# Query parts stored by whole column tile and loaded by SyncE, bias loads issued by ACT, the inversion's diagonal copies split over DVE and ACT

## The chip, the cores and the metric

The kernel runs on one core of a Trainium2 chip. The core has five engines that work through their own instruction queues in order: TensorE (PE, matrix products into PSUM; its weight loads are shown apart, as PEld), VectorE (DVE), ScalarE (ACT), GpSimd (POOL) and SyncE (SP, which here only issues transfers). Transfers between the chip's main memory and on-chip memory are run by 16 DMA engines, whoever issues them. The metric is the device time of one execution in microseconds. Before the change three runs took 1245.56, 1245.53 and 1241.6 us; the median is 1245.53.

## The reference

One layer of an encoder over 1024 tokens of width 1024, float32, with two groups of heads that read the same normalised input through one input projection: windowed attention (8 query heads of 64, 2 key heads, a band of 128 tokens to each side with a relative bias and a sink logit) and a gated delta rule that runs forwards and backwards (4 heads of 128). Then an output projection, a feed-forward block with squared ReLU and a final normalisation.

```python
xn = _rmsnorm(h, norm_mix_w[l])
proj = xn @ w_in[l]
q_a, k_a, v_a, qkv_g, z_g, a_g, b_g = jnp.split(proj, SPLIT_POINTS, axis=-1)
attn = _windowed_gqa(q_a, k_a, v_a, band_bias, in_window, attn_sink[l])
gdn = _gdn_mixer(qkv_g, z_g, a_g, b_g, conv_w[l], ...)
h = h + jnp.concatenate([attn, gdn], axis=-1) @ w_out[l]
hn = _rmsnorm(h, norm_ffn_w[l])
h = h + jnp.square(jax.nn.relu(hn @ w_ffn_in[l])) @ w_ffn_out[l]
...
# attention, per block n of 128 queries against its 3-block band of keys
scores = jnp.einsum("bnqkgd,bnskd->bnkgqs", qb, kb) * (ATTN_HEAD_DIM ** -0.5)
scores = scores + bias
probs = jax.nn.softmax(jnp.concatenate([scores, sink_col], axis=-1), axis=-1)[..., :-1]
...
# delta rule, per chunk
a_mat = jnp.where(strict, beta[..., :, None] * kk * decay, 0.0)
t_mat = lax.linalg.triangular_solve(eye + a_mat, eye, left_side=True, lower=True)
```

## The kernel before, in words

Most products are run as three: each operand is split into a rounded high part and the remainder, and PE adds high by high, high by low and low by high (L127 to L129). ACT makes the high part (L122 for weights, L501 for queries), POOL the low one (L123, L502).

The program is a chain of phases, in each of which generators are woven together. Around the change, from about 220 to 580 us, there are two such phases.

In the first, one stream runs the last input projections (`proj_conv`, `proj_z`, then `proj_attn`, whose last part makes the queries), and the other prepares the delta rule: `prep`, `eliminate`, `diag_blocks` and rounds 0 and 1 of `invert`. In the second, one stream is `attention`, then the output projection; the other runs rounds 2 and 3 of `invert`, then the scan forwards (`scan`, 8 chunks) and backwards.

**Queries.** For each key head `kv` two column tiles `i` of 128 columns (two heads each) and two halves of 512 tokens are projected. DVE evacuates the product (L500), ACT casts to the high part (L501), POOL subtracts (L502). Both parts are stored to a scratch tensor `qad` in main memory, since scores want the high part of a head on 64 partitions and the low part on the other 64 (the matching keys are laid out in the same way, in `kh` and `kl`). Before the change a store moves one head's part (64 partitions, L506): eight evacuations, 32 stores, all on SP. `query(n, kv)` loads the four heads of one block of 128 tokens as one tile; the load (L600) is issued by POOL. The first query of each key head is asked for while the projections still run, later ones two steps ahead.

**Attention.** A step is one block `n` and one key head `kv`, 16 in all: (0,0), (0,1), (1,0) and so on. PE makes scores (L550, L551), DVE adds the bias and finds the maximum (L552), ACT takes the exponentials (L564), DVE sums and scales (L565 to L569, one quarter of the scaling on POOL), PE transposes (L579), ACT evacuates (L581), and PE multiplies by the values (L591), which DVE evacuates (L594) and SP stores to `mad` (L595).

**Bias.** Four tiles of two heads each (`bias_table`), every one loaded by four transfers (L535) on SP. Their buffers come from the tag `pg`, 24 buffers which all large tiles share; the four were operands of the projections before.

**Inversion.** `invert` makes the inverse of a triangular 128 by 128 matrix per head, chunk and direction `d`, 8 of each direction at once, in four rounds `i`. The result tile is cleared by POOL (L716), the 32 by 32 diagonal blocks are copied in (L720, eight copies of 32 partitions by 256 elements, which read with a stride), a first product (L726) is copied to SBUF by ACT (L729), a second pair of products (L736, L740) gives the blocks beside the diagonal (L745, L752 on DVE), four more copies on ACT (L750) complete the 64 by 64 blocks, and two products of 64 (L759, copied by ACT at L761, then L767) give the last quarter (L770).

**Scan.** For each chunk SP loads `kvd` (L798), `pd` (L800) and for each pair of chunks `ktd` and `qtd` (L786); PE's products are at L805.

**What sets the order.** The streams are written as generators with due times, and the framework then orders the instructions by a simulated timeline, engine by engine: the order of each engine's queue is fixed when the program is built. Waits between engines are semaphores. Transfers issued by SP and ACT share eight completion counters in turn, so each transfer waits, on the queue that issues it, until the one eight places earlier in the program has landed.

Of the kernel before, what the change touches and what calls it, by code (L numbers as in the profile page):

```python
# [9 lines left out]
F32 = mybir.dt.float32  # L10
F32R = mybir.dt.float32r
# [5 lines left out]
P = 128  # L17
SEQ = 1024
# [3 lines left out]
HALF = 512  # L22
# [55 lines left out]
class Block:  # L78
# [389 lines left out]
    def proj_attn(self):  # L468


        nc = self.nc
# [7 lines left out]
        for i, half, ps in self.pair(raws):  # L479
            tok = slice(half * HALF, (half + 1) * HALF)  # L480
            t = self.pt()
# [14 lines left out]
        for kv in range(2):  # L496
            raws = self.load_w(self.w_cols(w, C_AQ + 256 * kv, 256))
            for i, half, ps in self.pair(raws):
                q, qh = self.pt(), self.pt(dt=F32R)
                nc.vector.tensor_scalar(out=q, in0=ps, scalar1=0.125, scalar2=None, op0=ALU.mult)  # L500
                nc.scalar.copy(out=qh, in_=q)  # L501
                nc.gpsimd.tensor_tensor(out=q, in0=q, in1=qh.bitcast(F32), op=ALU.subtract)  # L502
                for part, t in enumerate((qh.bitcast(F32), q)):
                    o = 64 * (kv ^ part)
                    for g in range(2):
                        nc.sync.dma_start(out=self.qad[kv, 2 * i + g, o:o + 64, half * HALF:(half + 1) * HALF],  # L506
                                          in_=t[64 * g:64 * g + 64, :])
                if i == 1 and half == 0:
                    self.qs.append(self.query(0, kv))
                yield 5.2  # L510
# [16 lines left out]
    def bias_table(self):  # L527
        self.bias = []
        for b in range(4):
            t = self.pg((P, 2, 3 * P))  # L530
            for m in range(4):
                src = bass.AP(tensor=self.biasd.tensor,
                              offset=self.biasd.offset + 2 * b * 32 * 512 + P - 1 - 32 * m,
                              ap=[[511, 32], [32 * 512, 2], [1, 3 * P]])
                self.nc.sync.dma_start(out=t[32 * m:32 * m + 32], in_=src)  # L535
            self.bias.append(t)

    def attn_scores(self, n, kv, mx, q, mk):
# [58 lines left out]
    def query(self, n, kv):  # L597

        q = self.pt((P, 4, P), F32R)
        self.nc.gpsimd.dma_start(out=q, in_=self.qad[kv, :, :, n * P:(n + 1) * P].rearrange("g c t -> c g t").bitcast(F32R))  # L600
        return q

    def attention(self):
# [91 lines left out]
    def invert(self, tt, steps):  # L695


        nc = self.nc
        blk = lambda q: slice(32 * q, 32 * q + 32)
        ct, ctt = self.ct, self.ctt  # L700
# [5 lines left out]
        for i in steps:  # L706
            ns = slice(8 * i, 8 * i + 8)
# [7 lines left out]
                tt[d][i] = mk((P, 2, GH, P), F32) if mk else self.pg((P, 2, GH, P))  # L715
                nc.gpsimd.memset(tt[d][i].rearrange("p c h x -> p (c h x)"), 0.0)  # L716
            t = [flat(tt[d][i]) for d in range(2)]
            for d in range(2):
                for q in range(4):
                    nc.scalar.copy(out=t[d][blk(q), :, blk(q)], in_=ctt[d][blk(q), :, ns].rearrange("p x n -> p n x"))  # L720
            px = self.ps("psB", (P, 8, 32))
            for n in range(8):
                for j in range(2):
# [2 lines left out]
                        nc.tensor.matmul(px[blk(e), n, :], at[d][blk(s), n, blk(e)], ct[d][blk(s), :, 8 * i + n],  # L726
                                         start=True, stop=True)
            x32 = self.pt((P, 8, 32))
            nc.scalar.copy(out=x32, in_=px)  # L729
            yield 1.4  # L730
            pyt, py = self.ps("psB", (P, 8, 32)), self.ps("psB", (P, 8, 32))
            for n in range(8):
                for j in range(2):
# [9 lines left out]
            for d in range(2):  # L743
# [4 lines left out]
                for q in (a, b):  # L748
                    c = slice(32 * (q % 2), 32 * (q % 2) + 32)
# [2 lines left out]
                nc.vector.tensor_scalar(out=t64[blk(b), :, 32 * (a % 2):32 * (a % 2) + 32], in0=py[blk(b)], scalar1=-1.0,  # L752
                                        scalar2=None, op0=ALU.mult)
            yield 2.4
            px = self.ps("psB", (P, 8, 64))
            for n in range(8):
                for d in range(2):
# [491 lines left out]
    def build(self):  # L1249
        tc, nc = self.tc, self.nc  # L1250
        with (
# [9 lines left out]
            self.hd, self.sd = d("hd", (NT, P, D))[:], d("sd", (DFF // 256, 7, P, HALF))[:]  # L1261
            self.gcd = dram.tile([3, 64, P], BF16, name="gcd")[:]
            self.zd, self.mad = d("zd", (GH, P, SEQ))[:], d("mad", (NT, P, HALF))[:]
            self.qad = d("qad", (2, 4, P, SEQ))[:]
            self.ktd, self.qtd = d("ktd", (GH, P, SEQ))[:], d("qtd", (GH, P, SEQ))[:]
            self.kvd = d("kvd", (NT, P, 2, GH, P))[:]
            self.pd, self.atd = d("pd", (NT, P, 2, GH, P))[:], d("atd", (NT, P, 2, GH, P))[:]
# [125 lines left out]
```

## Time and profile before

| | |
|---|---|
| median of three runs | 1245.53 us |
| profiled execution, its own time | 1245.29 us |
| its span, first to last instruction | 1243.6 us |
| mean granted TensorE clock | 0.983 |
| busy PE, PEld, DVE, ACT, POOL | 1179.3, 962.8, 854.0, 620.9, 574.4 us |
| stores L506, loads L535, loads L600 | 32, 16, 16, between 297 and 423 us |
| copies L720 | 32, between 263 and 347 us |

How to read the rows. A row of the timeline gives the start in us from the start of the span, the duration in us, the engine, the line of the kernel, the operation, destination and source tiles by name, the shape, how many instructions are merged into the row, and in square brackets the idle time before it with what ended that. A name with q behind the engine (SPq, ACTq) is the queue that issues a transfer; the row is the issuing, not the transfer. A row of the groups view gives, after the count, the busy time in us, the mean duration of one in ns, and the idle time before them with its causes. A cause is inferred from semaphores: where a wait has several, the latest one that the profile knows is named.

### The profile page before, as it was taken

The page shows a single profiled execution, that of the slowest core. Times are in us where ns is not written, and L with a number is a line of the kernel's source. Part 1 is how long each engine was busy: PE and PEld are TensorE (multiplying, and loading weights), DVE is VectorE, ACT ScalarE, POOL GpSimd, SP SyncE. Part 2 cuts the span into 40 slices and gives each one's busy share as a digit, 9 for nine tenths or more (in the row PEclk, how much of TensorE's full clock was granted, in tenths as well). Part 3 has the DMA queues.
Part 4 walks back from the last instruction along what each step waited for, and adds up shares of the span by engine and source line. Part 5 has one row for each costly group of instructions (what it writes and reads, how often), then busy time and mean ns, then how long its engine had stood idle before and what let it go on. Part 6 is the DMA issues. An engine that isn't in the chain of part 4 may idle for free. (4 is left out here: it accounts for less than half of the span.)

```text
span 1243.6 us, 18468 instructions
## 1 busy us (share of the span) xinstructions
PE 1179.3 (95%) x6482; PEld 962.8 (77%) x6482; DVE 854.0 (69%) x1466; ACT 620.9 (50%) x1347; POOL 574.4 (46%) x486
## 2 busy tenths in 40 slices
PE   6999999899879999997899999999999999999997
PEld 5788877778657778876788888888777888888885
DVE  4677667973378996677654453544579797887976
ACT  6455688354575752125464544545555433444343
POOL 5354312224422334234474535445365655665595
PEclk9999999899889999998999999999999999999999
DMA  6134344524746667222234444344679624434323
GB/s 240 52 117 141 104 167 140 180 81 135 172 145 172 168 220 263 96 83 84 86 120 154 151 153 144 144 158 147 214 263 320 235 84 155 152 133 138 98 89 136
DMA packets 121629, 187.62 MB, mean 151 GB/s; under 512 B 11043, under 2 KB 64416, under 8 KB 121537
## 3 DMA queue, kind: packets, MB, share of 16 engines
q1 hardware_dynamic: 96708, 152.58, 37.2%
q10 hardware_dynamic: 16381, 29.67, 6.2%
q0 software_dynamic: 8448, 4.20, 2.0%
q8 instruction: 51, 0.84, 0.3%
q14 instruction: 41, 0.34, 0.1%
HBM read 122.39 MB, written 63.49 MB: 149 GB/s over the span
## 5 line engine op out<-in xcount | busy, mean ns | idle before, releaser
L127 PE MATMUL psA<-pg,wh 128*128 128x512 f32 x416 | 164.8, 397 | 1.7 <-ACT pt L464 1.7
L129 PE MATMUL psA<-pg,wl 128*128 128x512 f32 x416 | 164.1, 395 | 0.0
L128 PE MATMUL psA<-pg,wh 128*128 128x512 f32 x416 | 163.7, 394 | 0.0
L123 POOL TENSOR_TENSOR wl<-wr,wh 128x512 fp32r<-128x512 f32 x44 | 66.7, 1536 | 159.6 <-ACT wh L122 129.4
L1168 DVE TENSOR_TENSOR pg<-pg 128x512 fp32r<-128x512 f32 x112 | 123.0, 1133 | 17.6 <-ACT pg L1167 17.6
L123 POOL TENSOR_TENSOR wh<-wr,wh 128x512 fp32r<-128x512 f32 x32 | 47.4, 1502 | 129.0 <-ACT wh L122 129.0
L128 PE MATMUL psA<-pg,pg 128*128 128x512 f32 x256 | 99.9, 392 | 0.4 <-POOL pg L123 0.3
L127 PE MATMUL psA<-pg,pg 128*128 128x512 f32 x256 | 99.3, 392 | 0.9 <-DVE pg L1213 0.9
L1085 ACT ACTIVATE pt<-pt 128x512 f32<-128x512 f32 x64 | 40.3, 632 | 119.3 <-DVE pt L1075 119.3
L129 PE MATMUL psA<-pg,pg 128*128 128x512 f32 x256 | 99.7, 390 | 0.0
L123 POOL TENSOR_TENSOR pg<-wr,pg 128x512 fp32r<-128x512 f32 x48 | 73.4, 1560 | 51.5 <-ACT pg L122 51.5
L127 PEld LDWEIGHTS psA<-pg,wh 128*128 128x128 f32 x416 | 78.6, 189 | 19.0 <-ACT pt L464 2.1
L128 PEld LDWEIGHTS psA<-pg,wh 128*128 128x128 f32 x416 | 78.6, 189 | 17.8 <-issue 0.9
L129 PEld LDWEIGHTS psA<-pg,wl 128*128 128x128 f32 x416 | 78.6, 189 | 16.8
L1167 ACT CAST pg<-pg 128x512 fp32r<-128x512 f32 x112 | 67.1, 620 | 40.4 <-DMA pg<-sd 29.3
L128 PE MATMUL psB<-pg,pg 128*128 128x512 f32 x192 | 74.9, 390 | 0.8 <-POOL pg L123 0.7
L129 PE MATMUL psB<-pg,pg 128*128 128x512 f32 x192 | 74.8, 390 | 0.2 <-DVE pg L1168 0.2
L127 PE MATMUL psB<-pg,pg 128*128 128x512 f32 x192 | 74.7, 389 | 0.0
L122 ACT CAST wh<-wr 128x512 fp32r<-128x512 f32 x76 | 43.6, 623 | 50.0 <-PE psA L128 30.0
L1075 DVE TENSOR_TENSOR pt<-psB,pt 128x512 f32<-128x512 f32 x39 | 26.9, 689 | 54.0 <-PE psB L129 29.5
L1075 DVE TENSOR_TENSOR pt<-psA,pt 128x512 f32<-128x512 f32 x39 | 26.8, 689 | 51.8 <-PE psA L129 36.3
L127 PEld LDWEIGHTS psA<-pg,pg 128*128 128x128 f32 x256 | 48.1, 188 | 12.6 <-DVE pg L1213 2.1
(395 smaller groups left out, 3265.3 us busy)
## 6 DMA issues: line engine op xcount, KB each, us to landing
sd<-pt ACTq DMA_DIRECT2D x112, 256.0 KB, 2.1
pg<-sd SPq DMA_DIRECT2D x112, 256.0 KB, 2.9
wr<-in_w_ffn_in SPq DMA_DIRECT2D x32, 512.0 KB, 3.6
wr<-in_w_in SPq DMA_DIRECT2D x22, 512.0 KB, 5.0
pg<-in_x SPq DMA_DIRECT2D x16, 512.0 KB, 6.7
wr<-in_w_ffn_out SPq DMA_DIRECT2D x16, 512.0 KB, 4.7
sc<-kvd SPq DMA_DIRECT2D x14, 512.0 KB, 6.0
kvd<-pt SPq DMA_DIRECT2D x16, 256.0 KB, 2.4
```

The lines of the kernel that those rows point to most:

```text
L122: nc.scalar.copy(out=h, in_=raw)
L123: (eng or nc.gpsimd).tensor_tensor(out=l, in0=raw, in1=h.bitcast(F32), op=ALU.subtract)
L127: nc.tensor.matmul(ps, wh, xh, start=first, stop=False, skip_group_check=onto)
L128: nc.tensor.matmul(ps, wh, xl, start=False, stop=False, skip_group_check=onto)
L129: nc.tensor.matmul(ps, wl, xh, start=False, stop=last, skip_group_check=onto)
L1075: self.nc.vector.tensor_tensor(out=out, in0=in0, in1=in1, op=ALU.add)
L1085: self.nc.scalar.activation(out=c, in_=c, func=AF.Relu)
L1167: nc.scalar.copy(out=s[:, 0], in_=raw)
L1168: v.tensor_tensor(out=s[:, 1], in0=raw, in1=s[:, 0].bitcast(F32), op=ALU.subtract)
```

## The change

Three edits. The scratch tensor gets the shape (key head, part, column tile, 128 columns, tokens), so that a store moves a whole column tile of one part (128 partitions, now L504, 16 stores), and `query` becomes two loads of 64 partitions, one for each part, issued by SP (still L600, 32 loads). The bias loads are issued by ACT (now L532). In `invert` the diagonal copies (now L722) of direction 1 are made by DVE, written after the first product's copy; those of direction 0 stay on ACT, written later and with an order edge that puts them behind that copy (now L732).

```diff
-                    o = 64 * (kv ^ part)
-                    for g in range(2):
-                        nc.sync.dma_start(out=self.qad[kv, 2 * i + g, o:o + 64, half * HALF:(half + 1) * HALF],
-                                          in_=t[64 * g:64 * g + 64, :])
+                    nc.sync.dma_start(out=self.qad[kv, part, i, :, half * HALF:(half + 1) * HALF], in_=t)
...
-                self.nc.sync.dma_start(out=t[32 * m:32 * m + 32], in_=src)
+                self.nc.scalar.dma_start(out=t[32 * m:32 * m + 32], in_=src)
...
-        self.nc.gpsimd.dma_start(out=q, in_=self.qad[kv, :, :, n * P:(n + 1) * P].rearrange("g c t -> c g t").bitcast(F32R))
+        for part in range(2):
+            o = 64 * (kv ^ part)
+            src = self.qad[kv, part, :, :, n * P:(n + 1) * P].rearrange("i (g c) t -> c (i g) t", c=64)
+            self.nc.sync.dma_start(out=q[o:o + 64].bitcast(F32), in_=src)
...
-            for d in range(2):
+
+            def diagonal(d):
                 for q in range(4):
-                    nc.scalar.copy(out=t[d][blk(q), :, blk(q)], in_=ctt[d][blk(q), :, ns].rearrange("p x n -> p n x"))
+                    out, src = t[d][blk(q), :, blk(q)], ctt[d][blk(q), :, ns].rearrange("p x n -> p n x")
+                    nc.vector.tensor_copy(out=out, in_=src) if d else nc.scalar.copy(out=out, in_=src)
+
             px = self.ps("psB", (P, 8, 32))
...
-            nc.scalar.copy(out=x32, in_=px)
+            moved = nc.scalar.copy(out=x32, in_=px)
             yield 1.4
+            diagonal(1)
...
             yield 2.4
+            with self.tc.issue_after(moved.ins):
+                diagonal(0)
...
-            self.qad = d("qad", (2, 4, P, SEQ))[:]
+            self.qad = d("qad", (2, 2, 2, P, SEQ))[:]
```

How the order moves, at the three places that matter below. Rows of the changed kernel carry its own line numbers: up to L500 they are the same, then the scores' exponentials L564 are L561, L729 is L732, L750 is L754, L798 is L804, L595 is L592.

ACT's queue before, from the fifth query cast to the exponentials of the second step; `wl` and `pg` are the inversion's result tiles of round 2 and then 3, `sc` the diagonal blocks:

```order
L720 COPY wl_3160<-sc_2267 32x8x32 x4
L501 CAST pt_2983<-pt_2982 128x512
L501 CAST pt_3023<-pt_3022 128x512
L501 CAST pt_3059<-pt_3058 128x512
L720 COPY pg_3163<-sc_2298 32x8x32 x4
L501 CAST pt_3093<-pt_3092 128x512
L729 COPY pt_3206<-psB_3173 128x256
L750 COPY pt_3295<-sc_2266 32x8x32 x2
L750 COPY pt_3295<-sc_2299 32x8x32 x2
L564 ACT_TABLE_LOAD
```

Behind the second step's exponentials there stand two more rows of four L720, ahead of the third step's. The same stretch of ACT's queue now:

```order
L501 CAST pt_2976<-pt_2975 128x512
L532 DMA pg_3087<-biasd 32x2x384 x4
L532 DMA pg_3092<-biasd 32x2x384 x4
L532 DMA pg_3097<-biasd 32x2x384 x2
L501 CAST pt_3014<-pt_3013 128x512
L532 DMA pg_3097<-biasd 32x2x384 x2
L532 DMA pg_3102<-biasd 32x2x384 x4
L501 CAST pt_3049<-pt_3048 128x512
L501 CAST pt_3081<-pt_3080 128x512
L732 COPY pt_3185<-psB_3152 128x256
L722 COPY wl_3147<-sc_2267 32x8x32 x4
L561 ACT_TABLE_LOAD
```

The sixteen bias loads stand among the casts, four diagonal copies of round 2 stand behind the first product's copy, the four copies L754 have moved behind the first step's exponentials, and no diagonal copy stands between the exponentials of the second and the third step any more.

POOL's queue before, from the second key head's first subtractions on (L716 clears an inversion result):

```order
L502 TENSOR_TENSOR pt_3022<-pt_3022,pt_3023 128x512
L600 DMA pt_3031<-qad 128x4x128
L716 MEMSET pg_3163 128x1024
L502 TENSOR_TENSOR pt_3058<-pt_3058,pt_3059 128x512
L600 DMA pt_3156<-qad 128x4x128
L502 TENSOR_TENSOR pt_3092<-pt_3092,pt_3093 128x512
```

The load that stands here before L716 is the second step's query, and it is now on SP. POOL's queue now:

```order
L502 TENSOR_TENSOR pt_3013<-pt_3013,pt_3014 128x512
L716 MEMSET pg_3150 128x1024
L502 TENSOR_TENSOR pt_3048<-pt_3048,pt_3049 128x512
L502 TENSOR_TENSOR pt_3080<-pt_3080,pt_3081 128x512
L755 MEMSET pt_3279 32x8x32 x2
```

No transfer stands among the subtractions any more, and the memset comes directly behind the second one of this key head.

SP's queue now, from the store of the second key head's second tile to the scan's second loads (before, the same place held stores and bias loads only, then L595 and the scan's loads):

```order
L504 DMA qad<-pt_3013 128x512
L600 DMA pt_3020<-qad 64x4x128 x2
L504 DMA qad<-pt_3049 128x512
L504 DMA qad<-pt_3048 128x512
L600 DMA pt_3142<-qad 64x4x128 x2
...
L600 DMA pt_3590<-qad 64x4x128 x2
L804 DMA sc_3720<-kvd 128x1024
L592 DMA mad<-pt_3485 128x512
L600 DMA pt_3672<-qad 64x4x128 x2
L792 DMA pg_3715<-ktd 128x4x256
```

The second step's query (`pt_3020`) stands directly behind its last store, the scan's first load (L804) behind the query of step (3,0) (`pt_3590`) and ahead of the first `mad` store, and the other loads of the scan behind the query of step (3,1) (`pt_3672`).

## The prediction, made before the changed kernel was run

> **What bounds the kernel now.** I read the page first, then the windows view, then the waits, then the timeline of each engine around the edited lines. The chain of waits on the page is of no use here: followed back from the end it stops at 837 us, and every edited line runs before 430 us. So the change must be read from its own stage.
>
> The windows view has, after the stretch and its length, the busy time of PE, PEld, DVE, ACT and POOL (instruction counts in brackets), the granted clock, the DMA share and GB/s:
>
> ```profile
> 300.00:320.00 20.00, 20.00 (x89) 16.54 (x89) 3.08 (x5) 6.20 (x10) 10.48 (x9) 1.00 0.68 175
> 320.00:340.00 20.00, 14.42 (x213) 11.51 (x211) 7.32 (x26) 10.12 (x21) 8.88 (x11) 0.89 0.83 197
> 340.00:360.00 20.00, 14.37 (x163) 10.01 (x164) 13.84 (x47) 17.34 (x45) 7.56 (x9) 0.69 0.14 26
> 360.00:400.00 40.00, 38.04 (x405) 32.08 (x404) 36.14 (x122) 22.98 (x69) 8.44 (x8) 1.00 0.68 194
> 400.00:440.00 40.00, 38.60 (x276) 31.22 (x276) 38.56 (x135) 27.45 (x77) 14.46 (x12) 1.00 0.66 184
> 480.00:520.00 40.00, 40.00 (x222) 34.72 (x221) 22.86 (x61) 4.99 (x19) 5.86 (x5) 1.00 0.39 135
> ```
>
> Up to 320 us the projections keep PE full. Between 320 and 360 PE is busy 28.8 of 40 us at a lowered clock, DVE is half idle, and after 340 ACT is the full engine (17.34 of 20). From 360 to 440 DVE is 90% and then 96% busy, and from 480 PE is full again. So the 40 us where the projections end and attention and the inversion begin are a hole; what comes after is bound by work, and starts earlier by whatever the hole shrinks.
>
> The timeline says what the hole waits for. First the query of the second step (steps are token block, then key head):
>
> ```profile
> 317.32 4.20 SPq L535 DMA_DIRECT2D pg<-biasd  x7
> 318.05 1.29 POOL L502 TENSOR_TENSOR pt<-pt,pt 128x512 f32<-128x512 f32 x1 [2.25 <-ACT pt L501]
> 321.62 2.37 SPq L506 DMA_DIRECT2D qad<-pt  x4
> 326.29 0.79 POOL L600 DMA_DIRECT2D pt<-qad  x1 [6.96 <-DMA qad<-pt]
> 328.08 2.53 ACT L720 COPY pg<-sc 32x256 f32<-32x256 f32 x4 [6.01 <-POOL pg L716]
> 331.57 0.36 PE L550 MATMUL psA<-pg,pt 128*128 128x256 f32 x1 [2.84 <-DMA pt<-qad]
> ```
>
> The low part is ready at 319.34 (318.05 + 1.29), but its store stands behind seven bias loads on SP until 321.62. POOL stands 6.96 us for the store to land; behind POOL's query load stand its memset L716, behind that ACT's diagonal copies (6.01), then a cast. PE gets the query at 331.57.
>
> Then the bias, and ACT:
>
> ```profile
> 332.63 0.58 SPq L535 DMA_DIRECT2D pg<-biasd  x1
> 336.93 0.42 DVE L552 CUSTOM_DVE_ANT_0 wr<-psA,pg 128x256 f32<-128x256 f32 x1 [3.96 <-DMA qad<-pt]
> 328.21 0.52 PE L726 MATMUL psB<-sc,dbl 32*32 32x32 f32 x24
> 331.16 0.37 ACT L729 COPY pt<-psB 128x256 f32<-128x256 f32 x1
> 331.43 2.81 ACT L750 COPY pt<-sc 32x256 f32<-32x256 f32 x4
> 335.55 0.51 ACT L564 ACTIVATE wr<-wr,nm 128x256 f32<-128x256 f32 x1
> 340.41 0.51 ACT L564 ACTIVATE wr<-wr,nm 128x256 f32<-128x256 f32 x1 [2.69 <-DVE nm L565]
> 342.49 5.20 ACT L720 COPY pg<-sc 32x256 f32<-32x256 f32 x8
> 347.70 0.62 ACT L564 ACTIVATE pg<-pg,nm 128x384 f32<-128x384 f32 x1
> 350.21 1.04 ACT L581 COPY pt<-psA 128x512 f32<-128x512 f32 x2
> 351.15 0.58 ACT L761 COPY pt<-psB 128x512 f32<-128x512 f32 x1
> 351.79 0.27 PE L767 MATMUL psB<-wl,pt 64*64 64x64 f32 x1 [3.28 <-ACT pt L761]
> ```
>
> DVE's wait of 3.96 is named after a store, but all stores it could need were long done; what ended just then is the last bias load, issued at 332.63. After that ACT sets the pace: the third step's exponentials start at 347.70 behind eight diagonal copies, the copy L761 comes behind those, and PE waits 3.28 us for it.
>
> **The change part by part.**
>
> *Stores and queries.* SP loses 16 of the 32 stores and 16 bias loads and gets 32 query loads. The view of one line gives duration in ns (least, median, most), first and last start, and under it the time to landing; the last row is ACT's own issuing, elsewhere in the kernel:
>
> ```profile
> L506 SPq DMA_DIRECT2D qad<-pt x32: 445/554/600, 297.6 to 333.8; - x32
> DMA to landing us min/median/max: 2.3/2.4/6.3
> L535 SPq DMA_DIRECT2D pg<-biasd x16: 371/426/1352, 317.3 to 332.6; - x16
> DMA to landing us min/median/max: 2.1/2.7/4.8
> L600 POOL DMA_DIRECT2D pt<-qad x16: 740/788/1001, 306.6 to 423.0; - x16
> DMA to landing us min/median/max: 3.3/4.5/9.0
> L1091 ACTq DMA_DIRECT2D sd<-pt x112: 325/326/1216, 633.3 to 945.6; - x112
> ```
>
> Issue time on SP: -16 x 0.554 - 16 x 0.426 + 32 x 0.43 to 0.55 = -2 to +2 us: nothing in sum. POOL is rid of 16 x 0.79 = 12.6 us, and of standing for stores. The second step's query: low part ready 319.3, store issued about 319.5, landed 2.4 to 3.9 later, say 323; load issued, landed about 3 us later (no row has this load; the bounds are 2.7, the bias rows, and 4.5, the same rows from POOL): 326 to 328 in place of 331.57. PE reaches those matmuls at about 328.7, so the 2.84 us go. Behind a query that waits on SP stand the remaining stores, which no step needs before the fifth token block, and the next queries, with one step to spare.
>
> *Bias.* Sixteen issues on ACT at 0.33 to 0.43 are 5.2 to 6.9 us. In the order they lie between the fifth and the seventh cast, in time 311 to 321.5; ACT is busy 6.20 us of the 20 to 320. They wait for operands of the projection to come free, whose last reader is the product that DVE evacuates at 316.58; it reads them one after the other, the four wanted in its first half, so the first issue is at about 312 and the fourth buffer free by about 314 (an estimate). Each also waits for the transfer eight places earlier. The last bias is issued at about 322 and there by 325 to 326, eleven us before 336.93. If the cover were missing, the seventh and eighth casts would be late first, and only queries of late blocks behind them.
>
> *Diagonal copies.* ACT loses 16 copies, DVE gets them:
>
> ```profile
> L745 DVE TENSOR_SCALAR pg<-psB 32x256 f32<-32x256 f32 x12 | 5.0, 418 | 6.7 <-PE psB L736 6.3 <-PE psB L740 0.3
> 342.53 0.87 DVE L569 TENSOR_SCALAR wr<-wr,nm 128x256 f32<-128x256 f32 x3
> ```
>
> On DVE no such copy is shown. From below: L569, equal in length, 0.29 each. From above: L745's 0.418 times 1.71, 0.71, because ACT takes 0.63 for this strided copy (2.53 / 4) and 0.37 for L729, which is as long and not strided. I take 0.5, so 2.0 us for four. Rounds 2 and 3 of the inversion put four each into 320 to 340, where DVE has 12.7 us idle; so zero on the path, 4 us if that idle time were gone.
>
> *The sum, along ACT's queue.* The first product of the inversion's round 2 ends at 328.73; in the new order ACT then does L729 0.37, four diagonal copies 2.53, the table load 1.31 (from 334.24, where L750 ends, to 335.55), the first step's exponentials 2.08 (340.41 to 342.49, the second step's), L750 2.81, the second step's exponentials 2.08. That ends at 339.9, where the third step's begin: 7.8 us before 347.70. They take 2.51 (347.70 to 350.21), two evacuations 1.0, and L761 follows at 343.4, against 351.15. The next edit takes some back: L750 of round 3 now stands behind four diagonal copies and gains only about 4.4:
>
> ```profile
> 355.34 2.56 ACT L750 COPY pt<-sc 32x256 f32<-32x256 f32 x4
> 363.65 0.42 DVE L752 TENSOR_SCALAR pt<-psB 32x256 f32<-32x256 f32 x1
> 277.78 0.33 PE L759 MATMUL psB<-pt,dbl 64*64 64x64 f32 x4 [0.92 <-POOL pg L490]
> ```
>
> L759 waits for both, and L752 was 6 us later (364.07 against 357.90), so this costs nothing. Upstream, in round 0 of the inversion, PE loses about 0.4 (20 projection matmuls no longer stand between the first product and the one that reads ACT's copy, L729's 0.37) and gains up to 0.92, the wait of the last row, since ACT's and DVE's inputs to L759 come earlier: between -0.4 and +0.5, I take +0.2. Sum 8.0 us (7.8 + 0.2) at 360, and DVE carries it on. The span of 1243.6 becomes 1235.6; around it lie 1.7 (the profiled execution took 1245.29), so 1237.3, and the median of 1245.53 is 0.24 above that execution: **1237.5**.
>
> A rule that speaks against this: the Trainium skill, "DMA: Bandwidth & Descriptors", section "Issuing engines are not separate DMA queues", says that transfers issued by several engines share the same 16 DMA engines, so another issuer saves only issue time. At the query's store that would be 321.62 - 319.34 = 2.3 us, not the 5 that I take; the trace cannot say yet, since its waits mix queue order and transfer.
>
> **The rivals.**
>
> *Half.* Transfers stay as slow as they are, since the DMA share of 0.68 to 0.83 is the same work in the same 40 us; only ACT's copies count. Then the second step's exponentials stay at 340.41, the third's follow at 342.49 without the eight copies, 5.2 earlier, and DVE's four copies of round 3, which stand ahead of the sums those need, take back about 1: 4.2 gained, **1241.3**. For it: stores landing after up to 6.3 us, queries after up to 9.0. Against it: the seven bias issues visibly ahead of the store, and POOL's 4.5 us for a query beside 2.4 to 2.7 for SP's transfers. The rule of the Trainium skill quoted above would end here.
>
> *Absorbed.* The scan's start, before:
>
> ```profile
> 359.22 0.74 POOL L600 DMA_DIRECT2D pt<-qad  x1 [1.08 <-PE psA L591]
> 360.17 1.24 SPq L798 DMA_DIRECT2D sc<-kvd  x1
> 369.10 0.49 PE L805 MATMUL psB<-sc,pg 128*128 128x128 f32 x2
> ```
>
> In the new order the scan's first load stands on SP behind the fourth block's first query, and its next loads behind the second one, which POOL issued at 359.22. If these queries stay where they are, so do the loads behind them and the scan's first product at 369.1, and DVE only does attention first: **1245**. For it: the coupling is new. Against it: those queries wait for buffers that the earlier steps free, and these move up too.
>
> *Slower.* ACT's bias loads form three turns in series, since each waits for the transfer eight places earlier, begun at about 313.5. With L for one landing the last lands at 314 + 3L, and DVE's reduction cannot pass it. At 2.7 to 4 that is 322 to 326; from L = 7.6 it is later than 336.93. At 9.0, the longest landing of a query, it is 341: DVE and ACT's exponentials start 4 us later than before, **1249.7**. For it: 0.83 of all DMA time is taken in that window. Against it: the median bias row landed in 2.7 in that same window.
>
> **How the numbers follow.** Two runs of this kernel differ by 0.3% without cause, 3.7 us. Forecast 0.52, with its own range 1233 to 1241; half 0.20; absorbed 0.14; slower 0.14. Half lies just past 0.3%: I give 0.12 of it to faster and 0.08 to same. Faster 0.52 + 0.12 = 0.64, same 0.14 + 0.08 = 0.22, slower 0.14. Below the forecast: 0.3 more upstream, and about 2 if PE no longer falls to the lower clock (0.69 in 340 to 360), with 3 of scatter: 1232. Above, the range takes in half and absorbed with a little scatter: 1246.5.
>
> **What would show it.** Right: PE's wait before the second step's scores gone; the last bias load there before 328; the third step's exponentials at about 340; L761 at 344; PE's wait of 3.28 gone; the scan's first product near 361. Wrong: ACT standing on a bias load past 323 (slower); query loads on SP landing after more than 6 us (half); the scan's first load still at 360 (absorbed); DVE's diagonal copies above 0.7 us, or ahead of a reduction that ACT waits for.

## The result, and the profile after

The changed kernel takes 1236.32 us (median of 13 runs, 1234.31 to 1241.54) against 1245.55 (13 runs of the kernel before beside them, 1241.6 to 1252.33): a ratio of 0.9929, 95% interval 0.9916 to 0.9942, so 8.8 us less (7.2 to 10.5). The forecast was 1237.5. The execution that was profiled is the slowest of the 13 (1241.54, span 1239.7); where it lost time is told below.

First the stage that the prediction was about. The windows view, before from the last evacuation of a query projection to the scan's first product, then the same stretch after (columns as in the prediction's first fence: PE, PEld, DVE, ACT, POOL, granted clock, DMA share, GB/s):

```profile
326.00:369.00 43.00, 31.64 (x545) 24.25 (x543) 28.65 (x101) 32.50 (x81) 17.34 (x21) 0.80 0.57 143
```

```profile
329.00:365.00 36.00, 28.51 (x548) 23.09 (x547) 29.91 (x105) 30.79 (x77) 10.10 (x12) 0.91 0.39 118
```

The same matrix work (545 and 548 products) takes 7 us less. PE is idle for 7.5 us where it was idle for 11.4, and its busy time falls by 3.1 us at a clock that falls less far (0.91 for 0.80). So in this pair of traces nearly half of what the hole gives back is clock. That fits the Trainium skill, "TensorE: Matmul & The Clock Gate", Part 1, by which an idle PE goes to half speed and comes back after some 3.4 us of work; the changed kernel's trace has such a piece from 275.0 to 278.4 us, at 0.50. The two parts do not go in step from one trace to the next: below, e1 stands idle for 7.4 us at a clock of 0.82, e2 for 7.9 at 0.91.

The exact edges of the hole, in the timelines, before and then after (the scan's first product of before, 369.10, stands in the prediction):

```profile
268.12 1.09 PE L726 MATMUL psB<-sc,dbl 32*32 32x32 f32 x64
326.16 0.69 DVE L500 TENSOR_SCALAR pt<-psA 128x512 f32<-128x512 f32 x1 [4.75 <-PE psA L129]
403.93 1.51 PE L591 MATMUL psA<-pt,pg 128*64 128x512 f32 x6 [1.40 <-ACT pt L581]
401.37 1.05 ACT L871 CAST wh<-pg 128x1024 fp32r<-128x1024 f32 x1 [1.42 <-DMA pg<-in_w_out]
```

```profile
269.17 1.09 PE L729 MATMUL psB<-sc,dbl 32*32 32x32 f32 x64
329.55 0.69 DVE L500 TENSOR_SCALAR pt<-psA 128x512 f32<-128x512 f32 x1 [4.67 <-issue]
364.79 1.16 PE L811 MATMUL psB<-sc,pg 128*128 128x128 f32 x8
395.53 1.05 ACT L877 CAST wh<-pg 128x1024 fp32r<-128x1024 f32 x1
```

From L500's last start to the scan's first product are 42.94 us before and 35.24 after: 7.70 us. A second piece lies at 402 us before, where ACT's cast L871 stands 1.42 us for a weight of the output projection, and PE 1.40 us for ACT's evacuation behind it. After, that cast waits for nothing. Together 7.7 + 1.4 = 9.1 us, about what the medians show.

The profiled execution shows less because it came into the hole late: 1.05 us at the first product of round 0 (L729; the granted clock from 10 to 30 us was 0.91 in this execution and 1.00 in the one before, far from the edits too), and 3.39 us at L500. The 2.3 us between are lost in round 0 of the inversion, on DVE, POOL and PE after:

```profile
269.47 3.76 DVE L722 COPY pg<-sc 32x256 f32<-32x256 f32 x4
273.26 0.69 DVE L482 COPY pt<-psA 128x512 f32<-128x512 f32 x1
269.80 2.65 POOL L123 TENSOR_TENSOR wl<-wr,wh 128x512 fp32r<-128x512 f32 x2 [2.90 <-ACT wh L122]
274.01 0.50 PE L127 MATMUL psA<-pg,wh 128*128 128x512 f32 x1 [1.85 <-DVE pt L482]
```

DVE's first four diagonal copies take 3.76 us, in rounds 1 to 3 only 1.5 to 1.7; L482 stands behind them, PE waits 1.85 us for it and then runs at the lower clock. The changed kernel is 5.8 us ahead at 440 us, 6.5 at 930 and 3.7 from 985 on; what is lost there lies far from the edits, and I did not follow it.

Inside the hole, the rows that answer to those of the prediction: ACT's and SP's queues, then PE.

```profile
314.08 4.79 ACTq L532 DMA_DIRECT2D pg<-biasd  x10
319.62 0.62 ACT L501 CAST pt<-pt 128x512 fp32r<-128x512 f32 x1 [5.04 <-DMA pg<-biasd]
319.64 2.80 ACTq L532 DMA_DIRECT2D pg<-biasd  x6
322.86 3.56 SPq L600 DMA_DIRECT2D pt<-qad  x2
331.92 0.37 ACT L732 COPY pt<-psB 128x256 f32<-128x256 f32 x1 [0.97 <-PE psB L729]
332.19 2.80 ACT L722 COPY wl<-sc 32x256 f32<-32x256 f32 x4
336.29 0.51 ACT L561 ACTIVATE wr<-wr,nm 128x256 f32<-128x256 f32 x1
338.36 2.50 ACT L754 COPY pt<-sc 32x256 f32<-32x256 f32 x4
342.97 0.60 ACT L561 ACTIVATE pg<-pg,nm 128x384 f32<-128x384 f32 x1
347.65 0.59 ACT L767 COPY pt<-psB 128x512 f32<-128x512 f32 x1
339.70 0.33 PE L765 MATMUL psB<-pt,dbl 64*64 64x64 f32 x2 [3.95 <-ACT pt L754]
```

All bias loads have left by 322.44. PE's waits of 2.84 (query) and 3.28 (L761, now L767) and DVE's of 3.96 are gone. In their place PE now waits 3.95 us for L754, which stands on ACT behind the diagonal copies and the first step's exponentials.

### The profile page after: what moved, and what is told of

Read it like the earlier page. It is cut to its first block, busy times and chain, and to the rows that moved or that the text cites. A ratio compares the mean times of both kernels' runs of the same rounds, so it can differ in the third digit from the quotient of the medians.

```text
span 1239.7 us, 18446 instructions
## 1 busy us (share of the span) xinstructions
PE 1178.8 (95%) x6482; PEld 964.3 (78%) x6482; DVE 856.8 (69%) x1482; ACT 611.3 (49%) x1331; POOL 560.7 (45%) x470
## 5 line engine op out<-in xcount | busy, mean ns | idle before, releaser
L123 POOL TENSOR_TENSOR wl<-wr,wh 128x512 fp32r<-128x512 f32 x44 | 66.3, 1527 | 157.3 <-ACT wh L122 129.5
L123 POOL TENSOR_TENSOR wh<-wr,wh 128x512 fp32r<-128x512 f32 x32 | 47.4, 1503 | 128.9 <-ACT wh L122 128.9
L123 POOL TENSOR_TENSOR pg<-wr,pg 128x512 fp32r<-128x512 f32 x48 | 72.5, 1540 | 52.7 <-ACT pg L122 48.8
L128 PEld LDWEIGHTS psA<-pg,wh 128*128 128x128 f32 x416 | 79.1, 190 | 18.1 <-issue 0.9
L128 PEld LDWEIGHTS psA<-pg,pg 128*128 128x128 f32 x256 | 48.4, 189 | 13.5 <-POOL pg L123 3.7
```

The source lines that it names most:

```text
L123: (eng or nc.gpsimd).tensor_tensor(out=l, in0=raw, in1=h.bitcast(F32), op=ALU.subtract)
L128: nc.tensor.matmul(ps, wh, xl, start=False, stop=False, skip_group_check=onto)
```

## The experiments

Each kernel ran 6 to 13 times and is compared with runs of the kernel before on the same chip, whose median lay between 1245.17 and 1246.30, so the ratios are what to compare. As a measure with less scatter than the total I take the hole, from L500's last start to the scan's first product, in the one trace of each kernel. Beside it stand two times counted from L500's last start: when the last bias load is issued, and when the third step's exponentials begin:

| kernel | last bias load | third exponentials | PE idle in the hole | hole, us | median, us | ratio to before (95%) |
|---|---|---|---|---|---|---|
| before | +6.5 | 21.5 | 11.4 | 42.9 | 1245.55 | 1 |
| f1_memset_dve | +6.3 | 22.7 | 10.9 | 42.2 | 1246.02 | 0.9998 (0.9982 to 1.0014) |
| g2_lowpart_dve | +3.0 | 17.6 | 8.6 | 38.0 | 1240.46 | 0.9960 (0.9945 to 0.9976) |
| e1_copies_only | +4.1 | 16.5 | 7.4 | 37.2 | 1242.57 | 0.9974 (0.9959 to 0.9990) |
| e2_bias_only | -1.9 | 16.2 | 7.9 | 36.5 | 1239.45 | 0.9958 (0.9943 to 0.9973) |
| e3_queries_only | -2.2 | 15.9 | 7.1 | 35.5 | 1238.11 | 0.9955 (0.9938 to 0.9973) |
| f2_bias_queries | -7.1 | 15.9 | 6.9 | 35.7 | 1237.69 | 0.9930 (0.9911 to 0.9949) |
| after | -7.6 | 13.4 | 7.5 | 35.2 | 1236.32 | 0.9929 (0.9916 to 0.9942) |
| g1_edge_no_split | -7.6 | 16.0 | 7.5 | 35.5 | 1238.86 | 0.9945 (0.9925 to 0.9966) |
| e4_round0_act | -7.1 | 13.4 | 7.5 | 35.4 | 1237.51 | 0.9943 (0.9926 to 0.9959) |
| e7_t64_early | -7.6 | 14.4 | 9.2 | 36.9 | 1239.03 | 0.9942 (0.9925 to 0.9960) |
| g3_edge_round3 | -7.4 | 12.7 | 6.0 | 33.2 | 1235.19 | 0.9909 (0.9884 to 0.9934) |
| e6_no_edge | -7.2 | 13.3 | 5.5 | 33.0 | 1234.29 | 0.9900 (0.9882 to 0.9917) |

### Each part alone

The three parts of the diff, one at a time on the kernel before.

> Before, with the diagonal copies' edit alone (four of eight on DVE, the other four on ACT behind the edge); stores, queries and bias loads as before. If the gain is the sum along ACT's queue, and each edit only takes its own piece of it: PE's wait for the second step's query (2.84 us at 331.57) and DVE's 3.96 us at 336.93 stay, the second step's exponentials stay near 340.4, and the third step's follow at 342.5 instead of 347.70, 5.2 us earlier; round 0 of the inversion shows the same 3.8 us of DVE copies ahead of L482 as the full change and loses about 2.5 us. Net 2 to 3 us: 1242.5 to 1243.5. If the copies alone carry the whole gain: 1236. If the loss in round 0 is an accident of the one profiled run: 1240.

> Before, with the bias loads issued by ACT and nothing else changed. Sum along ACT's queue: SP sends the second step's store about 2.3 us earlier, so PE's 2.84 us wait at 331.57 shrinks; the last bias load is issued by 324, so DVE's 3.96 us wait at 336.93 goes, the second step's exponentials move from 340.4 to about 338, and the eight diagonal copies still stand ahead of the third step's: 345 instead of 347.7. Gain 2 to 3 us: 1243. If bias loads on ACT hold up its casts, or form serial turns: slower, 1248. If copies alone carry the gain: 1245.5.

> Before, with the stores by whole column tile and the query loads on SP, nothing else changed. Sum along ACT's queue: POOL's memset L716 no longer stands behind a query load, so ACT's eight diagonal copies at 328.08 start up to 6 us earlier; but the bias loads stay on SP, the last of them is issued no earlier than 332.6, and DVE's wait at 336.93 for it stays, so the second step's exponentials stay near 340.4: gain 0 to 1 us here, and up to 1 us later in attention where POOL issued the queries: 1244 to 1245.5. If the issuing engine of the queries is what matters: 1241 or less.

Measured: 2.6 us, 5.7 and 7.1 by the medians (3.2, 5.2 and 5.6 by the ratios), 14 to 15 together where the whole change gives 9. So the parts are not pieces of a sum. e1's time came out as expected, e2 gave twice that, e3 fell to its rival (1241 or less). The hole shrank in all three by 5.7 to 7.4 us. In e1's case the one trace says more than its runs bear out: they spread from 1237.81 to 1245.12 and the profiled one is among the fastest.

A first theory for this was a ring of queues: bias loads on SP behind the last stores, these behind POOL's subtraction and ACT's cast, the cast behind ACT's diagonal copies, these behind POOL's memset, this behind POOL's query load, and that behind a store that stands behind bias loads on SP. If so, any one cut would free it. The next run cuts it at one instruction, on the kernel before:

```diff
-                nc.gpsimd.memset(tt[d][i]..., 0.0)
+                (nc.vector if (d, i) == (1, 2) else nc.gpsimd).memset(tt[d][i]..., 0.0)
```

> Before, with one instruction moved: the zeroing of the second diagonal's tile in round 2 (L716, 128x1024) is done by DVE and not by POOL. Stores, queries, bias loads and copies stay as before. Theory of the knot: before, a load of the bias on SP stands behind the last stores, these behind POOL's subtraction and ACT's cast, the cast behind ACT's diagonal copies, these behind POOL's L716, and that behind POOL's query load, which waits for a store that stands behind bias loads on SP; any cut of the ring lets it all go. Then ACT's wait of 6.01 us at 328.08 goes, its last cast is at about 326.5 and not 330.64, the last bias load is issued 3 to 4 us earlier, DVE's 3.96 us at 336.93 goes, and this alone is worth 3 to 5 us: 1240.5 to 1242.5; PE's 2.84 us at 331.57 stays. Sum of separate savings (each edit pays for what it takes away): nothing is taken away here, DVE gets about 1 us: 1245 to 1246.

Measured: 0.9998, nothing. Timelines of f1, ACT, POOL, SP and DVE:

```profile
321.71 2.69 ACT L720 COPY pg<-sc 32x256 f32<-32x256 f32 x4 [0.51 <-DVE pg L716]
326.02 0.62 ACT L501 CAST pt<-pt 128x512 fp32r<-128x512 f32 x1 [1.62 <-DVE pt L500]
326.01 0.79 POOL L600 DMA_DIRECT2D pt<-qad  x1 [7.54 <-DMA qad<-pt]
328.85 1.27 POOL L502 TENSOR_TENSOR pt<-pt,pt 128x512 f32<-128x512 f32 x1
331.57 0.58 SPq L535 DMA_DIRECT2D pg<-biasd  x1
337.20 0.42 DVE L552 CUSTOM_DVE_ANT_0 wr<-psA,pg 128x256 f32<-128x256 f32 x1 [5.93 <-DMA pg<-biasd]
```

ACT is free: its wait of 6.01 us has shrunk to 0.51, the last cast is at 326.02 and not 330.64. Yet the last bias load still leaves at 331.57, and DVE then waits 5.93 us, this time named after the bias itself. So ACT was no part of what holds the bias, and 6 us of waiting taken off ACT bought nothing. The theory that was left was a ring of SP and POOL: POOL's last subtractions stand behind its query load, which waits 7.54 us for a store, and SP's last stores and the last bias load would stand behind these. The next run cuts it at the subtraction, again on the kernel before:

```diff
-                nc.gpsimd.tensor_tensor(out=q, in0=q, in1=qh..., op=ALU.subtract)
+                nc.vector.tensor_tensor(out=q, in0=q, in1=qh..., op=ALU.subtract)
```

> Before, with the subtraction that makes the low part of a query (L502, eight of them) on DVE in place of POOL; nothing else. The ring without ACT in it (f1 took ACT out and the time stayed): the last bias loads on SP stand behind the last stores, these behind POOL's subtraction, and that behind POOL's query load, which waits 6 to 7 us for a store. Cut at the subtraction, the last store can leave about 2 to 3 us earlier, the last bias load is issued by 329 and not 332.63, DVE's wait at 336.93 for it shrinks by 3 us, DVE does 8 subtractions of about 0.7 us in its idle time: 1240 to 1242.5. If it is the issuing engine of the bias or of the queries that counts, and not the ring: 1245 to 1246.

Measured: 1240.46, inside what the second ring gives and outside its rival. SP, DVE and POOL in g2:

```profile
328.38 1.19 SPq L535 DMA_DIRECT2D pg<-biasd  x2
334.82 0.42 DVE L552 CUSTOM_DVE_ANT_0 wr<-psA,pg 128x256 f32<-128x256 f32 x1 [2.32 <-DMA qad<-pt]
325.12 0.79 POOL L600 DMA_DIRECT2D pt<-qad  x1 [13.94 <-DMA qad<-pt]
```

POOL still stands 13.94 us for a store, the last bias load leaves 3.0 us after L500's last start and not 6.5, and DVE's wait is 2.32 us (named after a store again). The number fits the ring, but SP's own rows in the kernel before do not. With the three that the prediction shows (317.32, 321.62 and 332.63) they are:

```profile
324.04 2.94 SPq L535 DMA_DIRECT2D pg<-biasd  x6
327.08 1.10 SPq L506 DMA_DIRECT2D qad<-pt  x2
328.23 1.35 SPq L535 DMA_DIRECT2D pg<-biasd  x1
329.68 1.08 SPq L506 DMA_DIRECT2D qad<-pt  x2
330.81 0.60 SPq L535 DMA_DIRECT2D pg<-biasd  x1
331.51 1.08 SPq L506 DMA_DIRECT2D qad<-pt  x2
```

Each row begins within 0.1 us of the end of the one before. From 313.58 to 334.40 SP issues 34 transfers one behind the other, 18 stores and 16 bias loads, with no gap above 0.10 us; in f1 it is the same 34 from 312.59 to 333.34, with none above 0.26. So in the kernel before SP waited there neither for POOL's subtractions nor for ACT's casts, and in f1 once for 0.26 us. The last bias load leaves late because it is the 32nd of a queue whose issuing alone fills the time. In the kernel before it landed 4.1 us later, 0.2 us before DVE starts at 336.93. In g2 only 27 issues fill that stretch up to the last bias load: two more stores have left before it, one bias load has gone into a pause ahead of it, and four stores and not two stand behind the last bias load. So g2 came inside its range by the order of SP's queue, and the ring is not shown. e2 takes the 16 bias loads off SP and e3 halves the stores, and in both SP's queue then has pauses again (up to 2.6 and 1.2 us).

e1 leaves SP's work alone, but the order of SP's queue came out another there as well:

```profile
327.79 1.53 SPq L535 DMA_DIRECT2D pg<-biasd  x3
335.25 0.42 DVE L552 CUSTOM_DVE_ANT_0 wr<-psA,pg 128x256 f32<-128x256 f32 x1 [1.12 <-DMA pg<-biasd]
341.32 0.62 ACT L564 ACTIVATE pg<-pg,nm 128x384 f32<-128x384 f32 x1 [0.29 <-DVE nm L559]
```

That is not where its gain comes from. Its last bias load leaves 2.4 us earlier against L500 than before, but lands only 0.3 us earlier (10.3 us after L500's last start, before 10.6), and DVE goes on with it hardly sooner. Behind that, in this trace, two things differ: the evacuations of the inversion's second products (L745 and L752 in the kernel before) now lie in DVE's wait and not behind it, so the second step's exponentials begin 2.8 us earlier, and no eight copies stand between them and the third step's. The third step's begin 16.5 us after L500's last start. The sum along ACT's queue gave 16.3 for this run (342.5), but with the second step's left where they were.

The table shows how this adds up. The hole follows the third step's exponentials from before down to e3: as long as these begin 16 us or more after L500, a later start is a longer hole, except that f1 and before change places. An earlier bias (e2, e3, g2) and e1's edit each bring them most of the way. Below 16 us the hole no longer follows them alone.

### What the copies' part adds

The full change without it:

> The full change without its third part: all diagonal copies on ACT as before. Theory of the knot: bias alone gave 5.7 us and queries alone 7.1; both cut the same ring, so together 7 to 8: 1237 to 1238, and the copies' edit adds 1 to 2 us at most in the full change. Sum along ACT's queue, as predicted: eight late copies (5.2 us) again stand ahead of the third step's exponentials, so 4 to 5 us are lost against the full change: 1240.5 to 1241.5. If savings added up: 1232.5.

Measured: 0.9930 against 0.9929, the hole 35.7 against 35.2. With the bias off SP and the query stores halved, the third part is worth nothing (the expectation's first branch gave 1 to 2 at most), against the 4 to 5 us of my sum along ACT's queue. ACT and PE in f2:

```profile
330.48 0.51 ACT L561 ACTIVATE wr<-wr,nm 128x256 f32<-128x256 f32 x1
337.19 5.18 ACT L720 COPY pg<-sc 32x256 f32<-32x256 f32 x8
342.38 0.61 ACT L561 ACTIVATE pg<-pg,nm 128x384 f32<-128x384 f32 x1
345.50 1.11 PE L576 MATMUL psA<-ident,wr 128*128 128x128 f32 x4 [3.22 <-ACT pt L578]
```

The eight copies stand ahead of the third step's exponentials, and PE waits 3.22 us at 345.50. In the changed kernel four of them stand ahead of the first step's exponentials, and PE waits 3.95 at 339.70. The part moved a wait from one place to another.

The part has two pieces, the split over two engines and the order edge. Taken apart, and the edge in round 3 alone:

```diff
 e6, from the changed kernel: direction 0 back ahead of the first product
+            diagonal(0)
             px = self.ps("psB", (P, 8, 32))
...
-            with self.tc.issue_after(moved.ins):
-                diagonal(0)
```

> The full change without the order edge: the first diagonal's four copies stay on ACT but stand where they stood, ahead of the round's first product. In the order this puts round 2's copies ahead of the sixth cast (about 320 us, where ACT is idle) and round 3's ahead of the third step's exponentials. If the edge does its part: third exponentials no earlier, 1236 to 1238 with 2.6 us of copies ahead of them. If what counts is only that four copies went to DVE: PE's 3.95 us wait for L754 at 339.70 falls to about 1.2 and L767 comes up to 2.8 us earlier: 1234.

```diff
 g1, from the changed kernel: no DVE, direction 1 on ACT ahead of the first product, direction 0 behind the edge
-                    nc.vector.tensor_copy(out=out, in_=src) if d else nc.scalar.copy(out=out, in_=src)
+                    nc.scalar.copy(out=out, in_=src)
...
+            diagonal(1)
             px = self.ps("psB", (P, 8, 32))
```

> The full change without DVE in it: all diagonal copies on ACT, the second diagonal's where they stood before, the first one's behind the order edge. With the full change (edge and split, 0.9929 of before), e6 (split alone, 0.9900) and f2 (neither, 0.9930) it makes a square. If the edge costs what the split gains, 3 to 4 us each: 0.996, 1240.5, with PE's wait for L754 near 339.7 as in the full change. If the edge costs only together with the copies on DVE: 0.993, 1237.

```diff
 g3, from the changed kernel
+            if i < 3:
+                diagonal(0)
...
+            if i == 3:
                 with self.tc.issue_after(moved.ins):
                     diagonal(0)
```

> The full change with the order edge in the inversion's round 3 alone; in rounds 0 to 2 the first diagonal's copies stand ahead of the first product. Round 2's four copies then lie in ACT's idle time near 315 to 320, as in e6, and round 3's are out of the way of the third step's exponentials. If ACT's queue sets the hole: third exponentials 2.5 us earlier than in e6, 1232. If DVE or PE set it by now: the same as e6, 1234.3. If round 3's first product waits for them: 1236.

A square: neither 0.9930, edge alone 0.9945, split alone 0.9900, both 0.9929. Only the split without the edge gains: about 3 us more than the full change. The two intervals still touch at their ends (0.9917 and 0.9916), but the hole is 2.2 us shorter, and 2.0 in g3, where rounds 0 to 2 have no edge. g1 shows no cost of the edge without the split, within its interval. e6's ACT and PE:

```profile
330.11 0.51 ACT L561 ACTIVATE wr<-wr,nm 128x256 f32<-128x256 f32 x1
332.19 2.52 ACT L755 COPY pt<-sc 32x256 f32<-32x256 f32 x4
339.38 0.62 ACT L561 ACTIVATE pg<-pg,nm 128x384 f32<-128x384 f32 x1
333.53 0.30 PE L764 MATMUL psB<-pt,dbl 64*64 64x64 f32 x2 [1.26 <-ACT pt L755]
338.15 0.69 PE L576 MATMUL psA<-ident,wr 128*128 128x128 f32 x2 [1.43 <-DVE wr L566]
```

Round 2's four copies lie at 306.9 to 309.7, where ACT is idle, so the first step's exponentials begin 4.1 us after L500's last start and not 6.7 as in the changed kernel, and PE has no wait above 1.43 us. g3 puts round 3's copies out of the way as well and is no faster than e6: its third exponentials begin 12.7 us after L500, e6's 13.3, and the hole is the same. So by then those exponentials no longer set the end, and that expectation of 1232 was missed.

The last one on ACT's queue moves other copies than the diagonal ones:

```diff
 e7, from the changed kernel: ct into t64 ahead of the round's first product, and no longer behind the second ones
+            t64 = self.pt((P, 8, 64))
+            for d in range(2):
+                for q in sub[d]:
+                    nc.scalar.copy(out=t64[...], in_=ct[d][...])
             px = self.ps("psB", (P, 8, 32))
```

> The full change, and each round's four copies of ct into t64 (L754) issued ahead of the round's first product, where ACT waits for the last projections, and not behind the first step's exponentials. If ACT's queue bounds the hole, as the sum has it: PE's 3.95 us wait for L754 at 339.70 falls to below 1.5, the third step's exponentials and L767 come 2.5 us earlier, and the time is 1.5 to 2.5 us below the full change: 1234 to 1235. If DVE's reductions or PE's clock bound it by now: the same as the full change, 1236 to 1237.

Measured: 1239.03, no gain (0.9942). PE's wait for L754 is gone, as expected, and a wait of 5.20 us for DVE's scaling of the first step's exponentials has taken its place:

```profile
335.35 1.11 PE L766 MATMUL psB<-pt,dbl 64*64 64x64 f32 x30 [0.83 <-DVE pt L757]
341.66 0.69 PE L576 MATMUL psA<-ident,wr 128*128 128x128 f32 x2 [5.20 <-DVE wr L566]
```

These transposes start 14.6 us after L500's last start, in the changed kernel 14.0 and in e6 12.1. So not L754 but the first step's exponentials hold them up, which in e7 still stand behind the four diagonal copies, and in e6 do not. Set side by side, the hole is 33 us only where the first step's exponentials begin about 4 us after L500's last start and the third step's before 13.5 (e6, g3); with the first early and the third at 15.9 (e3, f2) or the first at 6.7 and the third at 13.4 (after, e4) it is 35 to 36.

### Round 0

> The full change, but round 0's four copies of the second diagonal are back on ACT, ahead of the first product, where they were before. If DVE's copies ahead of L482 in round 0 cost what the two traces show (PE idle 1.85 us for L482 at 274.01 and a lowered clock at 275 to 278.4; the kernel is 3.6 us late at 281, of which 1.0 was there at 260): that wait and that cold window are gone, and the time is about 2.5 us below the full change, 1233.8. If what is lost at 281 is made up or lost again later by where the cold windows fall: 1236, the same as the full change.

(Its edit: for i equal to 0, direction 1 is copied by ACT ahead of the first product.) Measured: 1237.51, 0.9943, not the 1233.8 expected. The wait for L482 is gone from its trace, but the full change's runs do not pay for it on average. Other traces with the same four copies on DVE ahead of L482 say why: in e6 and f3 the copies are done before POOL's subtractions start, and PE does not wait.

> The full change with five more subtractions of 128x256 on POOL in the inversion's round 1 (of round 1's first product from itself, into a tile that nobody reads), beside DVE's four diagonal copies there. In round 0 these four took 3.76 us beside POOL's subtractions L123 and in rounds 1 to 3 1.5 to 1.7 us beside an idle POOL or a memset. If POOL's subtractions slow DVE's copies: round 1's four take 3 us or more. If round 0 has another reason (its tile, its transposes just before): 1.7 us as before.

DVE and POOL in f3, round 0 and then round 1, where L737 are the added subtractions:

```profile
267.37 1.59 DVE L722 COPY pg<-sc 32x256 f32<-32x256 f32 x4
269.05 2.51 POOL L123 TENSOR_TENSOR wl<-wr,wh 128x512 fp32r<-128x512 f32 x2 [2.89 <-ACT wh L122]
282.06 2.68 DVE L722 COPY pg<-sc 32x256 f32<-32x256 f32 x4
282.08 3.15 POOL L737 TENSOR_TENSOR scx<-pt 128x256 f32<-128x256 f32 x4 [1.88 <-ACT pt L732]
289.38 0.61 POOL L737 TENSOR_TENSOR scx<-pt 128x256 f32<-128x256 f32 x1
```

In round 0 the copies here take 1.59 us, done before POOL begins; in round 1, beside the added subtractions, 2.68 where the changed kernel took 1.68. That is below the 3 us expected but the theory's sign; POOL's four slow down too (up to 0.90 us, 0.61 alone). So POOL's subtractions slow DVE's copies, and round 0 costs something only in executions where the two meet. The Trainium skill, "SBUF — State Buffer", section "Who interferes with whom", says that a DVE copy in its two-port mode and a GpSimd instruction take a shared pair of ports whole, and the other waits. In the changed kernel the slowest copy, beside POOL's subtractions L123 (2.65 us for two), took 1.51 us against 0.39 in the median, which agrees. f3 ran once, for its trace alone.

## Why the prediction was right, and where it was not

*The number.* 1237.5 was forecast, 1236.32 measured. The hole was to shrink by 7.8 us and shrank by 7.7; the third step's exponentials were to begin 13.7 us after L500's last start (339.9 against 326.16) and begin after 13.4 (342.97 against 329.55); L761 17.2, measured 18.1; the scan's first product 34.9 at the forecast near 361, measured 35.2. L752, round 3's L750 and the rest cost nothing, as said.

*Query.* Right: the wait of 2.84 us is gone. The prediction set the rule of the Trainium skill, "DMA: Bandwidth & Descriptors", section "Issuing engines are not separate DMA queues", that another issuer saves only issue time, against itself. The runs are in keeping with it: sixteen issues of 0.43 us are 6.9 us, and e2, which edits nothing but the issuer of these 16 loads, gains 3 to 7. The section calls that time usually small; on SP's full queue it was not, 34 issues in a row took 20.8 us. "Half", which ended there, is excluded for the full change; 1242.57, the copies alone, lies near its figure.

*Bias.* Right in time (last issue 321.98; the loads whose landing the trace has took 2.2 to 4.1 us) and in that no serial turns hold DVE. The cast at 319.62 comes 5.04 us after ACT's last work, but the one behind it is no later than before (4.58 us ahead of L500's last start, before 4.71). "Slower" did not come, nor "absorbed": the scan's first load is at 356.98, not 360.

*Diagonal copies.* 0.5 us taken, 0.39 measured in the median, inside the bounds; beside POOL's subtractions up to 1.51, outside them. Hidden in rounds 1 to 3. The step "zero on the path" left out round 0, where four copies stand ahead of L482, and its price when POOL is busy: in the profiled execution the upstream term, taken as 0.2 us gained (bounds -0.4 and 0.5), was 2.3 lost.

*The sum along ACT's queue.* Here the amount was right, the path only in part, and the split into terms was not. That the hole follows the third step's exponentials holds in the table down to 16 us. But the sum gave 5.2 us of its 7.8 to the eight copies that no longer stand ahead of them. f2 keeps all eight there, its third exponentials begin 2.5 us later than the changed kernel's, and its hole is 0.4 us longer. f1 takes 6 us of waiting off ACT and gains nothing. Alone, the copies' part brings these exponentials 5.1 us forward (e1), but the bias loads alone bring them 5.3 forward (e2) and the queries alone 5.6 (e3), with every copy left on ACT: the parts overlap. What the sum left out is SP. The prediction saw DVE's wait of 3.96 us and named the last bias load behind it; it put SP's issue time at "nothing in sum" over all the stores and loads, where the bias stood in a stretch of 34 issues without a pause, and built its sum on the queue that comes after. So 1237.5 owes something to luck: the hole shrank by the forecast amount for reasons that the sum names only in part, and 1.4 us at 402 us and the loss upstream in the profiled execution were not in it.

*The edge.* The sum has round 2's four copies on ACT ahead of the first step's exponentials (2.53 us) as part of a gain. It did not ask where they would lie without the edge: in e6 and g3 ACT does them while it is idle, and the hole is 2 us shorter.

*Not foreseen.* The 1.4 us at 402 us, for which "DVE carries it on" had no term. The wait is gone in every kernel with the queries' part, e3 among them, and is there in every one without it (1.0 to 2.0 us in e1, e2, f1 and g2); why the weight lands earlier with the queries on SP was not tried.

*Open.* What sets the hole once the third step's exponentials begin before 16 us, beyond the side-by-side reading above; how much of e1's gain is the copies and how much the new order on DVE; and the scatter of e1's runs. Holes, clocks and starts come from one trace of each kernel.

## What to carry to other kernels

When a chain of waits runs through several in-order queues, find the transfer that ends last and look at its own queue before adding up the busy engine behind it. Where that queue issues without a pause, as SP's did here, its issue time is what to cut, whatever waits are to be seen on other engines: 6 us of waiting taken off ACT bought nothing here, and the same bias loads from another queue bought 5.7. If parts of a change overlap, try them singly and without each other; one that adds nothing may hide a piece that gains and a piece that gives it back, as here the split and the edge (e6, 1234.29, is the fastest kernel of this study). And read a hole twice: as idle time, and as the clock that it costs the work around it.

## What the runs showed of the hardware that was not expected

SP, which only issues, was a limit of its own: 34 transfers at 0.4 to 0.6 us, with two of 1.3, filled 20.8 us without a pause. DVE's strided copy of 32x256 takes 0.39 us and ACT's 0.65, but beside POOL's subtractions DVE's took up to 1.51, and POOL's of 128x256 went from 0.61 to as much as 0.90. A framework that orders by a simulated timeline turned an edit on ACT and DVE (e1) into another order on SP. And lowered clock can weigh nearly as much as idle time: 3.9 us less idle in the hole came with 3.1 us less busy time for the same products.
